# Z columns of a two-layer hybrid decoder: half of the contraction by a seven-product scheme

## The chip, the cores and the metric

The kernel runs on one core of one Trainium2 chip. The metric is the time of one execution in device microseconds. A core has a matrix engine (TensorE, PE; its weight loads are shown apart as PEld), a vector engine (VectorE, DVE), an activation engine (ScalarE, ACT), a general engine (GpSimd, POOL) and a synchronisation engine (SyncE, SP). Transfers are issued from the queues of SP, ACT or POOL and are carried out by 16 DMA engines that all queues share. SBUF holds tiles in 128 partitions; PSUM holds the results of matmuls, in eight banks of 128x512 f32.

## The reference, cut to what matters

256 tokens of width 2048 go through two layers. The second layer is an mLSTM; its input projection has columns for q and k, v, og (an output gate), z (a second gate) and two small gates. What the change touches is z and what is done with it:

```
hn  = rmsnorm(h, o_norm)
u   = hn @ o_w_in                       # [256, 2048] x [2048, 8208]
z   = u[..., 6144:8192]                 # 2048 columns
yc  = head_rmsnorm(mlstm(q, k, v, li, lf), c_norm) * sigmoid(og) * silu(z)
h   = h + yc @ o_w_out
pl  = rmsnorm(p[1] @ ple_w[1], ple_norm[1])
h   = h + sigmoid(h @ ple_gate_w[1]) * pl
out = rmsnorm(h, final_norm)
```

All is f32 with a tight tolerance, so the kernel makes each f32 product out of three matmuls of reduced precision.

## The kernel before, in words

**Products.** Every operand x is split into a high part (x rounded to the format of the fast matmul, made by a copy on ACT, L135 for weights) and a low part (x minus the high part, made on DVE, L136). A product is then high by high, high by low and low by high, three matmuls into the same PSUM bank (L196, L197, L198 in `quarter_tok`).

**Weights.** A weight matrix lies in HBM in blocks of 512 rows by 512 columns, 1 MB each, so that a block is one quarter `kq` of the contraction of one chunk `j` of columns. `load_weights` fetches a block in two halves of 512 KB through SP's queue into `raw` (five buffers, L132), and splits each half into `whi` and `wlo` (four buffers each, that is two blocks). The splits stand 400 places ahead in the order of their engines.

**A chunk.** `project_tok` walks over the four quarters; `quarter_tok` multiplies a block with both halves of the tokens (`hf`, 128 tokens each, stationary operand 128x128 from `act`, moving operand 128x512): 12 matmuls for each half, 24 for a block. After the first half `pump()` takes one step in every open lane of side work. The lanes are generators; what a step issues is queued behind the last matmul, cast and subtraction traced so far.

**The stage in question.** In the second layer the order is: q and k (`oqk`, 4 chunks), v (`ov`, 4), og (`oog`, 4), z (`oz`, 4), the embedding product `pw1` (L320), the output projection `oo`, the gate `g1`. The mLSTM itself runs in the lane "mix" beside `ov` and `oog`; its results `nums` wait in SBUF. For each of the four z chunks `gate_tok` evicts two PSUM banks: ACT makes tanh with the token's norm as scale (L522), DVE makes (tanh + 1) times z (L523), then two multiplications by the norm factor and `nums` (L1181). `feature_major` then turns the result from tokens to features: two transposes on DVE (L495), a store to DRAM and four reads back through POOL's queue (`across`, L482 and L485), a scaling on ACT (L513), and a split (L149 on ACT, L150 on DVE) into `y`, the operand of `oo`.

**The residual.** `hq`, four tiles of 128x1024, holds the layer's residual. It fills the four buffers of the pool `hp` (tag "h") from the end of the first layer until `out_proj` adds to it (L403). `ple_gate` writes it last; the lanes "fg0" to "fg3" turn it into `acth`, the operand of all four projections.

**Order.** A planner orders the instructions of each engine and each DMA queue by priority when the program is built; on the chip every engine and every queue works in that fixed order, and an instruction that waits holds what stands behind it on its engine. PSUM tiles: pool `pm` has three banks, `px` three, `pst` two.

Of the kernel before, what the change touches and what calls it, by code (L numbers as in the profile page):

```python
# [11 lines left out]
F32 = mybir.dt.float32  # L12
F32R = mybir.dt.float32r
# [30 lines left out]
def trunk(ctx: ExitStack, tc: tile.TileContext, a, out):  # L44
# [19 lines left out]
    def start(lane, gen):  # L64
        lanes.setdefault(lane, []).append(gen)
# [92 lines left out]
    def tokens(x, k, hf):  # L158
        return x[:, k, hf * P:(hf + 1) * P]
# [25 lines left out]
    def quarter_tok(w, j, kq, act, ps):  # L185

        parts = load_weights(w[4 * j + kq])
        for hf in range(2):
            for kk in range(4):
                k = kq * 4 + kk  # L190
                hi, lo = parts[kk // 2]
                c = (kk % 2) * 512
                ah, al, _ = act[k // 2]
                xh, xl = (tokens(x, k % 2, hf) for x in (ah, al))
                wh, wl = hi[:, c:c + 512], lo[:, c:c + 512]
                te.matmul(ps[hf], xh, wh, start=(k == 0), stop=False)  # L196
                te.matmul(ps[hf], xh, wl, start=False, stop=False)  # L197
                last["pe"] = te.matmul(ps[hf], xl, wh, start=False, stop=(k == KT - 1)).ins  # L198
            if hf == 0:
                pump()  # L200

    def newton(y, t, r, yh):
        v.tensor_scalar(t.bitcast(I32), y.bitcast(I32), 1, None, op0=ALU.logical_shift_right)
# [766 lines left out]
    with tc.tile_pool(name="m1", bufs=2) as m1:  # L970
# [188 lines left out]
                start("mix", mix_norm())  # L1159
        y = {}  # L1160
        held = []
        for j in range(4):
            ps = project_tok(a["oog"], j, acth)
            th = m1.tile([P, 2, 512], F32, name="tho", tag="vt", bufs=6)
            for hf in range(2):
                s.activation(th[:, hf], ps[hf], AF.Tanh, scale=norm["rth"][:, hf:hf + 1])
            held.append((j, th))
            if j == 3:
                drain("mix")
            for jj, th in [x for x in held if x[0] in nums]:  # L1170
                v.scalar_tensor_tensor(nums[jj], th, 1.0, nums[jj], op0=ALU.add, op1=ALU.mult)
            held = [x for x in held if x[0] not in nums]
        pact = load_p()
        for j in range(4):
            u = m1.tile([P, 2, 512], F32, name="u", tag="vt", bufs=6)
            gate_tok(a["oz"], j, acth, u)
            for hf in range(2):
                for i in range(2):
                    c = hf * 8 + 2 * j + i
                    e = slice(i * 256, (i + 1) * 256)  # L1180
                    v.scalar_tensor_tensor(u[:, hf, e], u[:, hf, e], fac[:, c:c + 1], nums[j][:, hf, e],  # L1181
                                           op0=ALU.mult, op1=ALU.mult)
            start(f"fm{j}", feature_major(u, "cn", 4 * j, y, 5))


        pairs = []
# [249 lines left out]
```

## Time and profile before

| What | Value |
|---|---|
| Median of 3 runs | 1035.66 us (1035.63 to 1035.77) |
| Span of the profiled execution | 1033.5 us, first to last instruction |
| Median less span | 2.2 us |
| TensorE busy | 1024.3 us, 99% of the span |
| VectorE busy | 739.6 us, 72% |
| ScalarE busy | 600.1 us, 58% |
| GpSimd busy | 90.3 us, 9% |
| Share of PE in the chain that ended last | 98% |
| z chunks, first matmul to the embedding's first matmul | 752.5 to 839.6 us |

The page gives no time of its own for the profiled execution beside its span. A busy engine is one with an instruction in work; matmuls overlap, so their durations add up to more than the time they take, and the distance between starts is what one costs. The chain that ended last is followed back from the last instruction, at each step to what released it.

### The profile page before, as it was taken

The numbers are of one execution on the slowest core, as the hardware profiler recorded it, in microseconds if no ns is written. First come the engines' busy times: TensorE is split into PE (matmuls) and PEld (weight loads), VectorE is DVE, ScalarE is ACT, GpSimd is POOL, SyncE is SP. The second block draws the span as 40 slices with busy tenths as digits, with TensorE's granted clock in tenths as the row PEclk, the third lists the DMA queues.
The fourth block names the chain that finished last, engine by engine and source line by source line (L and its number), as shares of the span: only waits on it lengthen the run. The fifth ranks groups of instructions, "written<-read, shape, count | busy, mean of one in ns | idle before, by whom it ended". The sixth has DMA issues, their size and how long they took to land.

```text
span 1033.5 us, 14411 instructions
## 1 busy us (share of the span) xinstructions
PE 1024.3 (99%) x5230; PEld 851.2 (82%) x5230; DVE 739.6 (72%) x1130; ACT 600.1 (58%) x863; POOL 90.3 (9%) x170
## 2 busy tenths in 40 slices
PE   9999999999999999999999999999999999999996
PEld 8888888888888888888888888888888888888886
DVE  7858968969685776767569986755557776766684
ACT  7675555586964444565557875654445557344562
POOL 0111101011111111111021000000001111111000
PEclk9999999999999999999999999999999999999999
DMA  9987756567688897697597655456567777788652
GB/s 364 327 238 238 224 165 204 185 195 240 227 258 296 274 282 235 213 276 230 191 268 244 221 184 173 155 180 194 187 201 228 250 252 247 221 286 269 202 184 82
DMA packets 67656, 234.79 MB, mean 227 GB/s; under 512 B 8801, under 2 KB 10209, under 8 KB 67585
## 3 DMA queue, kind: packets, MB, share of 16 engines
q1 hardware_dynamic: 55584, 196.51, 58.3%
q0 software_dynamic: 11568, 36.84, 12.5%
q8 instruction: 41, 0.67, 0.3%
q10 hardware_dynamic: 432, 0.52, 0.1%
q14 instruction: 31, 0.25, 0.1%
HBM read 216.02 MB, written 17.83 MB: 226 GB/s over the span
## 4 chain that ended last, share of the span: by engine, by line
PE 98%; ACT 1%; DMA 1%; DVE 0%; issue 0%; ACTq 0%
PE mm L196 27%; PE mm L197 27%; PE mm L198 27%; PE mx L198 4%; PE mx L197 4%; PE mx L196 4%; PE mm L320 1%; PE nu L1118 1%; DMA raw<-in_pw_dram 1%; PE mm L1262 1%; PE mm L1261 1%; PE mm L1260 1%; PE mx L632 0%; PE mx L756 0%; PE mx L1098 0%; ACT whi L135 0%
## 5 line engine op out<-in xcount | busy, mean ns | idle before, releaser
L136 DVE TENSOR_TENSOR wlo<-raw,whi 128x1024 fp32r<-128x1024 f32 (+1 forms) x357 | 431.3, 1215 | 222.0 <-ACT whi L135 209.5
L135 ACT CAST whi<-raw 128x1024 fp32r<-128x1024 f32 (+1 forms) x357 | 373.5, 1049 | 323.8 <-PE mm L198 265.7
L196 PE MATMUL mm<-whi,ahl 128*128 128x512 f32 x1216 | 474.8, 391 | 0.0
L197 PE MATMUL mm<-wlo,ahl 128*128 128x512 f32 x1216 | 473.6, 389 | 0.1
L198 PE MATMUL mm<-whi,ahl 128*128 128x512 f32 x1216 | 473.2, 389 | 0.0
L196 PEld LDWEIGHTS mm<-whi,ahl 128*128 128x128 f32 x1216 | 228.3, 188 | 48.0 <-issue 0.8
L197 PEld LDWEIGHTS mm<-wlo,ahl 128*128 128x128 f32 x1216 | 228.3, 188 | 47.5 <-DVE wlo L136 0.9
L198 PEld LDWEIGHTS mm<-whi,ahl 128*128 128x128 f32 x1216 | 228.3, 188 | 47.4
L196 PE MATMUL mx<-whi,ahl 128*128 128x512 f32 x160 | 62.2, 389 | 0.0
L197 PE MATMUL mx<-wlo,ahl 128*128 128x512 f32 x160 | 62.2, 389 | 0.0
L198 PE MATMUL mx<-whi,ahl 128*128 128x512 f32 x160 | 62.2, 389 | 0.0
L197 PEld LDWEIGHTS mx<-wlo,ahl 128*128 128x128 f32 x160 | 30.0, 188 | 6.3
L196 PEld LDWEIGHTS mx<-whi,ahl 128*128 128x128 f32 x160 | 30.0, 188 | 6.3
L198 PEld LDWEIGHTS mx<-whi,ahl 128*128 128x128 f32 x160 | 30.0, 188 | 6.1
L482 POOL DMA_DIRECT2D ducn<-w x4 | 2.2, 560 | 214.7 <-DVE w L495 214.7
L995 DVE SCALAR_TENSOR_TENSOR qk<-xr,prm,qk 128x255 f32<-128x255 f32 (+2 forms) x48 | 20.4, 471 | 0.1
L150 DVE TENSOR_TENSOR ahl<-xr,ahl 128x512 fp32r<-128x512 f32 x24 | 16.3, 685 | 4.5 <-ACT ahl L149 4.4
L149 ACT CAST ahl<-xr 128x512 fp32r<-128x512 f32 x24 | 14.7, 612 | 4.2 <-DVE xr L844 4.0
L366 DVE STREAM_TRANSPOSE w<-hq 128x512 f32<-128x512 f32 x24 | 16.7, 702 | 0.2
L384 DVE TENSOR_TENSOR ahl<-r,ahl 128x128 fp32r<-128x128 f32 x64 | 13.9, 279 | 2.9 <-ACT ahl L382 2.9
L320 PE MATMUL mm<-whi,ahl 128*128 128x512 f32 x48 | 14.9, 389 | 0.0
L382 ACT CAST ahl<-r 128x256 fp32r<-128x256 f32 x32 | 10.6, 402 | 7.5 <-DMA r<-dfo 4.7
(332 smaller groups left out, 827.5 us busy)
## 6 DMA issues: line engine op xcount, KB each, us to landing
raw<-in_ew_dram SPq DMA_DIRECT2D x64, 512.0 KB, 5.5
raw<-in_g_dram SPq DMA_DIRECT2D x64, 512.0 KB, 4.7
raw<-in_eo_dram SPq DMA_DIRECT2D x32, 512.0 KB, 5.5
raw<-in_oqk_dram SPq DMA_DIRECT2D x32, 512.0 KB, 4.7
raw<-in_ov_dram SPq DMA_DIRECT2D x32, 512.0 KB, 4.2
raw<-in_oog_dram SPq DMA_DIRECT2D x32, 512.0 KB, 4.0
raw<-in_oz_dram SPq DMA_DIRECT2D x32, 512.0 KB, 4.4
raw<-in_oo_dram SPq DMA_DIRECT2D x32, 512.0 KB, 4.8
```

The costliest lines, as they stand in the source:

```text
L135: last["act"] = s.copy(h, r).ins
L136: last["dve"] = v.tensor_tensor(out=l, in0=r, in1=h.bitcast(F32), op=ALU.subtract).ins
L149: (v.tensor_copy if name == "p0" else s.copy)(hi, src)
L150: v.tensor_tensor(out=lo, in0=src, in1=hi.bitcast(F32), op=ALU.subtract)
L196: te.matmul(ps[hf], xh, wh, start=(k == 0), stop=False)
L197: te.matmul(ps[hf], xh, wl, start=False, stop=False)
L198: last["pe"] = te.matmul(ps[hf], xl, wh, start=False, stop=(k == KT - 1)).ins
L320: last["pe"] = te.matmul(ps[hf][:, o:o + w_], tokens(pact[x], k, hf), (hi, lo)[y][:, k * 512 + o:k * 512 + o + w_], start=(n == mine[0]), ...
L366: v.transpose(w5[:, hf], h[:, hf].rearrange("p (c j q) -> p c j q", c=4, j=4))
L382: s.copy(hk, src)
L384: v.tensor_tensor(out=lk[:, hf], in0=src[:, hf], in1=hk[:, hf].bitcast(F32), op=ALU.subtract)
L995: v.scalar_tensor_tensor(dst[:, sh:T], pi[:, 0:T - sh], pc("ccw", k * 16 + n), dst[:, sh:T], op0=ALU.mult, op1=ALU.add)
```

## The change

The four z chunks are worked in two pairs (chunks 0 and 1, then 2 and 3). Quarters 2 and 3 of the contraction go on as before (`plain`, 24 matmuls a block). Quarters 0 and 1 of both chunks of a pair form a product of 2x2 blocks: two halves of tokens by two quarters, times two quarters by two chunks. These eight block products become seven (`seven`), by sums of blocks on both sides.

On the weights' side the sums are made in SBUF: the chain tile X is loaded with block (chunk 0, quarter 0), and then (1, 0), (1, 1) and (0, 1) are added to it by transfers from POOL's queue that accumulate into their destination; Y is loaded with (1, 1), and (1, 0) is added. Between two additions the present value is split into high and low parts. On the activations' side `combos` makes four combinations once, from `acth`, in a lane beside `oog`, and keeps them split in four tiles `q4`, which take the four buffers of `hp`. So `hq` is stored to DRAM after `ple_gate` and read back after the z chunks. The results are put together by partial sums in four tiles `pr` (one ACT copy and six DVE operations a pair), and the gate's operations read three of four results from SBUF instead of PSUM.

```
+    def product(o, stat, parts, first=False, end=False):
+        for k in range(4):
+            xh, xl = (x[:, k] for x in stat)
+            wh, wl = (x[:, (k % 2) * 512:(k % 2 + 1) * 512] for x in parts[k // 2])
+            for n, (x, y) in enumerate(((xh, wh), (xh, wl), (xl, wh))):
+                last["pe"] = te.matmul(o, x, y, ...).ins
+    def combos(act, qs):
+        def whole(i, j):
+            x = tp.tile([P, 512], F32, name="xr", tag="hn", bufs=3)
+            for b in range(2):
+                h, l = act[2 * j + b][0:2]
+                o = x[:, b * T:(b + 1) * T].rearrange("p (k t) -> p k t", k=2)
+                v.tensor_tensor(out=o, in0=tokens_of(h, i), in1=tokens_of(l, i), op=ALU.add)
+            return x
+        def keep(n, x):
+            q = hp.tile([P, 1024], F32R, name="q4", tag="h")
+            s.copy(q[:, 0:512], x)
+            v.tensor_tensor(out=q[:, 512:1024], in0=x, in1=q[:, 0:512].bitcast(F32), op=ALU.subtract)
...
+    def seven(w, j, act, qs, room, rest):
...
+        def add(chain, b, kq):
+            for hf in range(2):
+                gp.dma_start(out=chain[hf], in_=src(b, kq, hf), accum_op=ALU.add)
...
+        X = begin(0, 0, room)
+        parts = split(X)
+        add(X, 1, 0)
+        product(A, quadrant(act, 0, 0), parts, True)
+        p1 = part()
+        urgent(s.copy, p1, A)
+        Y = begin(1, 1, room)
+        parts = split(Y)
+        add(Y, 1, 0)
+        product(E, qs[4], parts, True)
+        plain(w, j, 2, act, (A, F), first=(False, True))
+        parts = split(X)
+        add(X, 1, 1)
+        product(B, qs[1], parts, True)
+        p15 = part()
+        urgent(v.tensor_tensor, out=p15, in0=B, in1=p1, op=ALU.add)
+        plain(w, j, 3, act, (A, F))
+        parts = split(X)
+        add(X, 0, 1)
+        product(B, qs[2], parts)
+        g = part()
+        urgent(v.tensor_tensor, out=g, in0=B, in1=p1, op=ALU.subtract)
+        parts = load_weights(w[4 * j + 1])
+        product(A, quadrant(act, 1, 0), parts, end=True)
+        yield 0, 0, A
+        pump()
+        parts = split(Y)
+        product(B, qs[3], parts)
+        urgent(v.tensor_tensor, out=p15, in0=B, in1=p15, op=ALU.subtract)
+        parts = split(X)
+        product(F, quadrant(act, 1, 1), parts, end=True)
+        urgent(v.tensor_tensor, out=p15, in0=F, in1=p15, op=ALU.subtract)
+        yield 0, 1, p15
+        pump()
+        plain(w, j + 1, 2, act, (E, B))
+        plain(w, j + 1, 3, act, (E, B), end=True)
+        urgent(v.tensor_tensor, out=g, in0=E, in1=g, op=ALU.add)
+        yield 1, 0, g
+        urgent(v.tensor_tensor, out=p1, in0=B, in1=p1, op=ALU.subtract)
+        yield 1, 1, p1
...
     acth = ple_gate(hq, a["g0"], act, pls, rp0, hss0, "on", "fg", ready(act, "fe"), gate_sums)
+    away = []
+    for c in range(4):
+        d = dr.tile([P, 2, 512], F32, name=f"dh{c}")
+        gp.dma_start(out=d, in_=hq[c])
+        away.append(d)
...
+        qs = {}
+        start("combos", combos(acth, qs))
         for j in range(4):
             ps = project_tok(a["oog"], j, acth)
...
+        drain("combos")
         pact = load_p()
-        for j in range(4):
-            u = m1.tile([P, 2, 512], F32, name="u", tag="vt", bufs=6)
-            gate_tok(a["oz"], j, acth, u)
-            for hf in range(2):
+        for jj in (0, 2):
+            us = [m1.tile([P, 2, 512], F32, name="u", tag="vt", bufs=6) for _ in range(2)]
+            for b, hf, src in seven(a["oz"], jj, acth, qs, chain_room, part_room):
+                j, u = jj + b, us[b]
+                with tc.high_priority(offset=100):
+                    s.activation(u[:, hf], src, AF.Tanh, scale=norm["rth"][:, hf:hf + 1])
+                    v.scalar_tensor_tensor(u[:, hf], u[:, hf], 1.0, src, op0=ALU.add, op1=ALU.mult)
...
+                if hf:
+                    start(f"fm{j}", feature_major(u, "cn", 4 * j, y, 5))
+        hq = []
+        for c in range(4):
+            t = hp.tile([P, 2, 512], F32, name="hq", tag="h")
+            gp.dma_start(out=t, in_=away[c])
+            hq.append(t)
```

X and Y lie in the four buffers of the tag "qk" (`chain_room`); the products of a pair run in the order P1 (X with one block), Y1, quarter 2 of chunk j, X2, quarter 3 of chunk j, X3, quarter 1 of chunk j, Y2, X4, and quarters 2 and 3 of chunk j + 1.

More of the change, by code (lines that the diff above doesn't have):

```diff
@@ L200, in quarter_tok, with split_weights @@
                 pump()
+    def split_weights(r):
+        hi, lo = (wp.tile([P, 1024], F32R, name=n, tag=n) for n in ("whi", "wlo"))
+        with tc.high_priority(offset=400):
+            last["act"] = s.copy(hi, r).ins
+            last["dve"] = v.tensor_tensor(out=lo, in0=r, in1=hi.bitcast(F32), op=ALU.subtract).ins
+        return hi, lo
+    def product(o, stat, parts, first=False, end=False):
[3 more added lines that the diff above has]
+            for n, (x, y) in enumerate(((xh, wh), (xh, wl), (xl, wh))):
+                last["pe"] = te.matmul(o, x, y, start=(first and k + n == 0), stop=(end and k == 3 and n == 2),
+                                       skip_group_check=True).ins
```

52 lines of the change are left out of this document (51 added, 1 removed).

## The prediction

> **What bounds the kernel now.** I read the busy shares on the page first, then the chain that ended last and the granted clock.
>
> ```profile
> span 1033.5 us, 14411 instructions
> PE 1024.3 (99%) x5230; PEld 851.2 (82%) x5230; DVE 739.6 (72%) x1130; ACT 600.1 (58%) x863; POOL 90.3 (9%) x170
> PE 98%; ACT 1%; DMA 1%; DVE 0%; issue 0%; ACTq 0%
> core 0: 1033.5 us, clock 0.998
> ```
>
> TensorE is busy 99% of the span at full clock and is 98% of the chain, so a matmul taken away is worth its spacing as long as nothing else makes PE wait. What one is worth, and where the z columns lie, comes from the groups by line between 752.7 and 839.6 us, two rows of the timeline of PE, and one row of the chain in order of time.
>
> ```profile
> L196 PE MATMUL mm<-whi,ahl 128*128 128x512 f32 x128 | 49.8, 389 | 0.0
> 768.01 0.39 PE L196 MATMUL mm<-whi,ahl 128*128 128x512 f32 x1
> 773.45 0.39 PE L196 MATMUL mm<-whi,ahl 128*128 128x512 f32 x1
> 839.57 10.88 PE mm L320 x48
> ```
>
> The 389 ns overlap. From 768.01 to 773.45 there are 24 starts, so a matmul costs 0.2267 us. L196, L197 and L198 have 128 each: 384 matmuls, 87.05 us, which run without a gap from 752.5 to the first L320 at 839.57. Now the other engines in that stage, in four stretches of one chunk each: PE, PEld, DVE, ACT, POOL busy us (instructions), clock, DMA share, GB/s.
>
> ```profile
> 752.70:774.50 21.80, 21.80 (x98) 18.06 (x97) 12.56 (x13) 9.75 (x11) 0.00 (x0) 1.00 0.62 194
> 774.50:796.20 21.70, 21.70 (x98) 17.96 (x97) 14.00 (x17) 9.66 (x11) 2.74 (x5) 1.00 0.78 242
> 796.20:818.00 21.80, 21.80 (x98) 18.06 (x97) 15.08 (x19) 12.39 (x17) 2.74 (x5) 1.00 0.80 241
> 818.00:839.60 21.60, 21.60 (x97) 17.90 (x96) 14.80 (x19) 12.09 (x16) 2.74 (x5) 1.00 0.77 242
> sum 86.90, PE 86.90 PEld 72.00 DVE 56.44 ACT 43.89 POOL 8.22; mean PE 21.73 PEld 18.00 DVE 14.11 ACT 10.97 POOL 2.06
> ```
>
> DVE has 30 us of room in the stage, ACT 43, and the transfers run at 0.6 to 0.8 of the engines. These three pay for the change.
>
> **PE: what goes.** Per pair of chunks, 16 products of 12 matmuls become 15; no other matmul is added. Twelve per pair, 24 in all, by 0.2267 us: 5.44 us (2.72 per pair). A product is 2.72 us, a pair 40.8 instead of 43.5, the stage 81.6. This is the whole possible gain, 0.53%.
>
> **Splits.** Per pair, 8 blocks of weights were split (two halves each); now 11, since a Strassen block serves one product instead of two. The cost of one, from the groups by line of the stage and the timeline of DVE:
>
> ```profile
> L135 ACT CAST whi<-raw 128x1024 fp32r<-128x1024 f32 x34 | 35.9, 1055 | 37.3 <-PE mm L198 37.2
> L136 DVE TENSOR_TENSOR wlo<-raw,whi 128x1024 fp32r<-128x1024 f32 x32 | 38.6, 1218 | 28.2 <-ACT whi L135 26.7
> 774.67 2.32 DVE L136 TENSOR_TENSOR wlo<-raw,whi 128x1024 fp32r<-128x1024 f32 x2
> 772.40 0.69 DVE L523 SCALAR_TENSOR_TENSOR u<-u,mm 128x512 f32<-128x512 f32 x1 [1.20 <-ACT u L522]
> 773.12 0.88 DVE L1181 SCALAR_TENSOR_TENSOR u<-u,fac,num 128x256 f32<-128x256 f32 x2
> 801.42 0.65 DVE L150 TENSOR_TENSOR ahl<-xr,ahl 128x512 fp32r<-128x512 f32 x1
> L403 DVE TENSOR_TENSOR hq<-mm,hq x12: 679/684/692, 335.6 to 938.4; 128x512 f32<-128x512 f32 x12
> ```
>
> The casts idle for PE's L198: each waits only for a slot of whi, four slots being two blocks. So a half is ready 1.06+1.22 = 2.28 us after PE lets its slot go. Six more blocks are 12 halves: ACT 12.7, DVE 14.6 us (13.9 back to back, 1.16 each). The partial sums add six DVE operations per pair between PSUM and SBUF, nearest L403: 12 by 0.684 is 8.2, and one ACT copy per pair. DVE then has 56.4+14.6+8.2 = 79 us in 81.6, ACT 58. On average DVE just fits; the narrow place is the four single products in a row (X3, kq1 of j, Y2, X4), 10.9 us. There DVE has 8 halves by 1.16 (9.3), two partial sums (1.4) and the first token half's gate (0.69+0.88): 12.2. The 1.3 over is covered by lead: a slot is free 1.5 products (4.08 us) before its half is due, which leaves 1.8. In the second pair fm0's sixth step falls on the explicit pump after kq1 and brings two of L150, 1.3, into the same place: 0.8 over. I take 0.2 for the first pair and 0.8 for the second, **1.0 us**; ends are 0 (all absorbed) and 5.2 (both pairs exceed by the whole 1.3+1.3, twice).
>
> **Activation combinations, spill, reload.** Work in the stages before and after, from the groups by form of DVE and the stretches by window:
>
> ```profile
> L384 DVE TENSOR_TENSOR ahl<-r,ahl 128x128 fp32r<-128x128 f32 x64 | 13.9, 279 | 2.9 <-ACT ahl L382 2.9
> 690.00:710.00 20.00, 20.00 (x90) 16.54 (x89) 9.31 (x8) 9.02 (x9) 0.00 (x0) 1.00 0.64 202
> 485.01 2.19 POOL L485 DMA_DIRECT2D r<-dfg  x4 [3.41 <-DMA dfg<-w]
> 518.13 0.56 POOL L482 DMA_DIRECT2D dqk<-w  x1 [30.93 <-DVE w L978]
> ```
>
> The combinations are 8 adds of 128x256 (between 0.28 and 0.68, say 0.45) and 8 operations of 128x512 (0.68): 9 us of DVE, once for both pairs, in the stage whose DVE is busy 9.3 in 20: no cost; without that cover 9 us. The spill is four stores of 512 KB on POOL's queue behind the last of fg's reads at 485; POOL's next issue is dqk at 518, after 31 idle us. The reload is asked for when the q4 tiles are free, about 13 us before the z columns end, and first read over 40 us later. On POOL it stands ahead of fm3's transfer, which is due only at the last quarter of oo's first chunk. Both cost nothing unless they slow SP's loads, which have five buffers; bounds 0 to 2 us. On SP's queue the second pair's first loads wait until X4 and Y2 are split (25 to 27 us into the first pair) and are split themselves from 34 on; behind them stand that pair's kq2 and kq3, due later still.
>
> **The accumulating transfers** are the unknown. Per pair four blocks, two 512 KB transfers each, on POOL's queue; each waits for the split that read the old value, and the next split waits for it. From the DMA issues, a stretch at the program's head and the timeline of POOL:
>
> ```profile
> raw<-in_oz_dram SPq DMA_DIRECT2D x32, 512.0 KB, 4.4
> ducn<-w POOLq DMA_DIRECT2D x4, 512.0 KB, 3.4
> row<-in_rows_dram POOLq DMA_DIRECT2D x6, 512.0 KB, 7.6
> xt<-in_x_dram SPq DMA_DIRECT2D x4, 512.0 KB, 9.4
> 8.00:16.00 8.00, 8.00 (x37) 6.54 (x35) 5.21 (x8) 7.02 (x13) 0.00 (x0) 1.00 1.02 410
> 801.79 0.56 POOL L482 DMA_DIRECT2D ducn<-w  x1 [16.07 <-DVE w L495]
> 805.80 2.18 POOL L485 DMA_DIRECT2D r<-ducn  x4 [3.45 <-PE mm L198]
> ```
>
> How long may one take? Count from the pair's first product. P1 0, Y1 2.7, kq2 5.4, X2 10.9, kq3 13.6, X3 19.0, kq1 21.8, Y2 24.5, X4 27.2, then kq2 and kq3 of j+1 to 40.8. X2's slots come free in Y1's product, so its halves are split by 6.4 and 7.7. X4's must begin to be split by 24.9 and 26.3 (2.28 before use). Between lie 18.5 us, less X3's own split 2.3: 16.2 for two adds, **8.1 us each** from issue to landing. The first add of the chain has more room (X1's split ends near -3, X2 is due at 8.6). Beyond 8.1, each us costs 2 per pair, 4 in all; the gain of 4.4 is gone at 9.2.
>
> Bounds: below by a plain SP load in this stage, 4.4 (not below: the bytes are the same); above by the slowest plain 512 KB that the run shows, xt with 9.4, plus 1.3 us for the destination (a sum has to read what it adds to: 0.52 MB at 410 GB/s): 10.7, which costs 10.4 us. I take the load 4.4 plus 1.3, plus 1.4 because the halves follow one another 1.36 us apart and share the queue: **7.1 us**, no stall. I choose the oz row as the nearest because its source, shape and stage are the same; row's 7.6 comes from pairs issued together beside small packets.
>
> DMA load: the stage moves 20.0 MB now (the four GB/s by their lengths). Six more block transfers of 1.05 MB make 26.3 in 81.6 us, 322 GB/s against 410 at the head: fits. The Trainium skill ("Collectives: The Full Stack", Stop ④) describes an add inside a transfer as read-read-write. By that eight adds read 8.4 MB more: 34.7 MB, 425 GB/s by that rule, above what the head sustained, and the sum would be that of the first rival; no row of this kernel shows an add.
>
> The sum: -5.44 + 1.0 = -4.4. The profiled execution's span is 1033.5, so 1029.1 there; the median of the runs is 1035.66, 2.2 above the span, so **1031.2**.
>
> **The rivals.**
> (1) *The adds land late; slower.* Place: X3, then X4. The point of decision is 9.2 us from issue to landing. For it: xt's 9.4 under full queues, and the destination's bytes would bring the stage to the head's rate. Against: loads here land in 4.4. At 10.7: 1031.2 + 4 x 2.6 = 1041.6; at 12, 1046.8. A POOL queue in which X3's add stands behind a transposition's reads (issue to reads 4.0, plus 2.18) adds up to 6 us in the second pair alone.
> (2) *DVE becomes the bound.* 79 us in 81.6 is 97%. If its order costs 3 to 6% the stage is 82 to 84 and the upper end of 5.2 applies: 1035.4, no change. For it: partial sums and gates need PSUM quickly and sit among the splits. Against: measured busy times overlap by 5% back to back.
> (3) *The change doesn't do what it says:* a spare matmul or a PE gap at the stage's ends takes half the gain, 1033. Against: 15 products can be counted in the code.
>
> **How the numbers follow.** 0.2% is 2.07 us, about what can be told from no change. The forecast, with (3) and small stalls (1030 to 1033.5), 0.50. Rival 2, or adds at 8.7 to 9.7 (1033.6 to 1037.7), 0.18. Rival 1, 0.32, of which 0.1 above 1045. The range 1030 to 1045 leaves out that 0.1 and a few hundredths below. The forecast's own range is 1030 to 1033.5.
>
> **What would show it.** Right: 360 matmuls of 0.2267 between the first z matmul and L320's successor, 81.6 to 83 us; chain still PE; POOL's adds landing under 8.1 us; DVE near 95% there. Wrong: weight loads of PE waiting for the split of X3 or X4, whose cast waits for the accumulating transfer (rival 1); or waiting for DVE's split while ACT's cast was long done (rival 2); a slower oqk or oo stage would contradict the spill at nothing.

## The result, and the profile after

| | Before | After |
|---|---|---|
| Median | 1035.64 us | 1048.31 us (1046.24 to 1051.18) |
| Ratio to before, 95% interval | | 1.0123 (1.0103 to 1.0143) |
| Span of the profiled execution | 1033.5 us | 1047.9 us |
| z chunks, first matmul to the embedding's first | 87.05 us | 97.18 us |
| Embedding, first matmul to the output projection's first | 10.88 us | 11.90 us |

The change made the kernel slower by 1.2%, where 0.4% faster was forecast. From the page of the changed kernel: the span, the busy engines, the issues of the accumulating transfers (count, KB, median us to landing), and the shares of the chain that ended last.

```profile
span 1047.9 us, 14475 instructions
...
PE 1025.5 (98%) x5206; PEld 848.4 (81%) x5206; DVE 764.6 (73%) x1170; ACT 613.6 (59%) x881; POOL 109.3 (10%) x194
...
PE 78%; issue 12%; DMA 6%; ACT 1%; DVE 1%; POOL 1%; ACTq 0%; POOLq 0%; SPq 0%; DVEq 0%
...
ch<-in_oz_dram POOLq DMA_DIRECT2D x16, 512.0 KB, 7.1
```

PE has its 24 matmuls less (5206 for 5230), yet its share of the chain fell from 98 to 78%. DMA has 6% of the chain now, and 12% are put down to "issue", time in which the engine waited for nothing that the profile shows. The fourth row is a trap: the median landing of the 16 accumulating transfers is 7.1 us, by chance to the digit what the prediction took for each, and the stage still lost 15.6 us against the 81.6 that 360 matmuls need.

The timeline of PE in the changed kernel shows where. Rows: start, us, instruction, and in brackets the idle time of the engine before it and what ended it.

```profile
754.91 0.39 PE L216 MATMUL mm<-whi,ahl 128*128 128x512 f32 x1
...
776.86 0.50 PE L216 MATMUL mm<-wlo,q 128*128 128x512 f32 x1 [0.76 <-DVE wlo L207]
...
817.28 0.39 PE L216 MATMUL mx<-whi,ahl 128*128 128x512 f32 x1
824.84 0.80 PE L216 MATMUL mm<-whi,q 128*128 128x512 f32 x1 [7.18 <-ACT whi L206]
826.11 0.79 PE L216 MATMUL mm<-wlo,q 128*128 128x512 f32 x1 [0.47 <-DVE wlo L207]
...
831.04 0.40 PE L216 MATMUL mm<-whi,ahl 128*128 128x512 f32 x1
...
838.58 0.50 PE L216 MATMUL mx<-wlo,ahl 128*128 128x512 f32 x1 [1.35 <-DVE wlo L207]
...
852.09 0.39 PE L457 MATMUL mm<-whi,ahl 128*128 128x512 f32 x1
```

L206 and L207 are the cast and the subtraction of the chain tiles, so these are the splits of X3 and X4. X3 of the first pair costs 1.3 us (between 775 and 777), X3 of the second pair 7.3 us (817.28 to 824.84, where 0.23 is due), X4 of the second pair 1.6. And X3's 12 matmuls then take 6.20 us (824.84 to 831.04) instead of 2.72, of which 0.47 is one more wait, for a subtraction. The cast that PE waited for, in ACT's timeline, and its cause in the chain of waits:

```profile
823.75 1.04 ACT L206 CAST whi<-ch 128x1024 fp32r<-128x1024 f32 x1 [13.14 <-DMA ch<-in_oz_dram]
```

```profile
810.63 0.56 POOL ch L284
811.19 15.37 DMA ch<-in_oz_dram
```

ACT sat idle 13.14 us until an accumulating transfer landed; the transfer of the other half was in flight for 15.37 us. Why X3's two additions were asked for only at 810.6 is seen in POOL's timeline of the second pair:

```profile
801.39 0.85 POOL L284 DMA_DIRECT2D ch<-in_oz_dram  x1 [2.63 <-DVE wlo L207]
805.49 2.26 POOL L622 DMA_DIRECT2D r<-ducn  x4 [3.25 <-DMA ducn<-w]
807.74 0.94 POOL L284 DMA_DIRECT2D ch<-in_oz_dram  x1
810.07 0.58 POOL L619 DMA_DIRECT2D ducn<-w  x1 [1.39 <-DVE w L632]
810.63 1.79 POOL L284 DMA_DIRECT2D ch<-in_oz_dram  x2
```

Y's second addition (807.74) stood behind a transposition's four reads, which waited for their store to land; X3's two stood behind the next chunk's store, which waited for its transpose. X2 had been split by 807.4, so they were 3.3 us late at the start. The landing itself, first of all 16, then by the time of issue X3 of the first pair (762 to 766) and X3 of the second (810 to 813):

```profile
DMA to landing us min/median/max: 5.6/7.1/15.4
...
DMA to landing us min/median/max: 7.7/9.4/11.0
...
DMA to landing us min/median/max: 13.0/14.2/15.4
```

Four windows of the changed kernel, two with additions in flight, one with the first pair's gap and one with the second's (last three columns: granted clock, DMA share, GB/s):

```profile
762.00:774.00 12.00, 12.00 (x55) 9.94 (x54) 5.38 (x5) 3.16 (x3) 2.55 (x3) 1.00 1.04 279
805.00:817.00 12.00, 12.00 (x54) 9.94 (x54) 7.71 (x11) 2.27 (x3) 5.55 (x8) 1.00 1.04 246
770.00:780.00 10.00, 9.12 (x40) 6.96 (x39) 6.24 (x6) 6.22 (x7) 1.70 (x2) 1.00 0.87 216
820.00:830.00 10.00, 4.69 (x9) 2.94 (x10) 3.49 (x3) 4.39 (x5) 3.92 (x7) 0.52 0.95 193
```

The DMA engines are full at 246 to 279 GB/s, where the head of the program reached 410 at nearly the same share (1.02). In the last row the granted clock is 0.52: that is most of why X3's matmuls took 6.2 us. The Trainium skill ("TensorE: Matmul & The Clock Gate", Part 1) says that an idle window of about 3.4 us puts the clock to half. This trace fits that: 0.52 comes after a gap of 7.2 us, and the first pair's gap of 1.3 us left the clock at 1.00 (third row). Two of the runs below do not: where the transposition was kept away the clock went to 0.50 (818.3 to 820 us) after a gap of 2.0, and with one pair spaced it stayed at 1.00 (840 to 850 us) through gaps of 3.4 and 2.0. So the length of a gap does not tell by itself.

Of the span's 14.4 us, 10.1 lie in the z chunks and 1.0 in the embedding. The stage also began at 754.91 instead of 752.5. That comes in the main from the head of the program, where nothing was changed: from 6 to 12 us the granted clock was 0.72 in this profile and 1.00 in that of before. In the runs below the start moves between 752.0 and 754.3, so I do not count these 2.4 us to the change. The last 0.9 lie behind.

### The profile page after: what moved, and what is told of

It is laid out like the page before. It is cut to its first block, busy times and chain, and to the rows that moved or that the text cites. A ratio compares the mean times of both kernels' runs of the same rounds, so it can differ in the third digit from the quotient of the medians.

```text
span 1047.9 us, 14475 instructions
## 1 busy us (share of the span) xinstructions
PE 1025.5 (98%) x5206; PEld 848.4 (81%) x5206; DVE 764.6 (73%) x1170; ACT 613.6 (59%) x881; POOL 109.3 (10%) x194
## 4 chain that ended last, share of the span: by engine, by line
PE 78%; issue 12%; DMA 6%; ACT 1%; DVE 1%; POOL 1%; ACTq 0%; POOLq 0%; SPq 0%; DVEq 0%
PE mm L196 20%; PE mm L197 20%; PE mm L198 20%; DMA ch<-in_oz_dram 4%; PE mx L197 3%; PE mx L196 3%; PE mx L198 3%; PE mm L216 2%; DMA hq<-dh 1%; DMA r<-ducn 1%; PE mm L1423 1%; PE mm L1422 1%; PE mm L1421 1%; PE mx L457 1%; PE mm L457 1%
## 5 line engine op out<-in xcount | busy, mean ns | idle before, releaser
L136 DVE TENSOR_TENSOR wlo<-raw,whi 128x1024 fp32r<-128x1024 f32 (+1 forms) x345 | 415.7, 1215 | 187.4 <-ACT whi L135 176.2
L135 ACT CAST whi<-raw 128x1024 fp32r<-128x1024 f32 (+1 forms) x345 | 359.7, 1047 | 284.8 <-PE mm L198 221.5
L196 PE MATMUL mm<-whi,ahl 128*128 128x512 f32 x1088 | 425.1, 391 | 0.2 <-ACT pl L469 0.2
L197 PE MATMUL mm<-wlo,ahl 128*128 128x512 f32 x1088 | 423.5, 389 | 0.0
L198 PE MATMUL mm<-whi,ahl 128*128 128x512 f32 x1088 | 423.4, 389 | 0.0
L196 PEld LDWEIGHTS mm<-whi,ahl 128*128 128x128 f32 x1088 | 204.2, 188 | 43.8 <-issue 0.8
L198 PEld LDWEIGHTS mm<-whi,ahl 128*128 128x128 f32 x1088 | 204.3, 188 | 42.6
L197 PEld LDWEIGHTS mm<-wlo,ahl 128*128 128x128 f32 x1088 | 204.3, 188 | 41.5
L207 DVE TENSOR_TENSOR wlo<-ch,whi 128x1024 fp32r<-128x1024 f32 x24 | 28.7, 1220 | 26.0 <-ACT whi L206 25.7
L206 ACT CAST whi<-ch 128x1024 fp32r<-128x1024 f32 x24 | 24.9, 1050 | 31.4 <-DMA ch<-in_oz_dram 23.6
L216 PE MATMUL mm<-whi,ahl 128*128 128x512 f32 x128 | 40.9, 389 | 0.0
L284 POOL DMA_DIRECT2D ch<-in_oz_dram x16 | 13.9, 893 | 179.7 <-DVE wlo L207 179.7
L216 PE MATMUL mm<-whi,q 128*128 128x512 f32 x64 | 23.1, 422 | 7.3 <-ACT whi L206 7.2
L216 PEld LDWEIGHTS mm<-whi,ahl 128*128 128x128 f32 x128 | 24.0, 188 | 5.0
L216 PE MATMUL mm<-wlo,ahl 128*128 128x512 f32 x64 | 25.0, 391 | 0.7 <-DVE wlo L136 0.7
```

Of the source, the lines that this page charges most:

```text
L135: last["act"] = s.copy(h, r).ins
L136: last["dve"] = v.tensor_tensor(out=l, in0=r, in1=h.bitcast(F32), op=ALU.subtract).ins
L206: last["act"] = s.copy(hi, r).ins
L207: last["dve"] = v.tensor_tensor(out=lo, in0=r, in1=hi.bitcast(F32), op=ALU.subtract).ins
L216: last["pe"] = te.matmul(o, x, y, start=(first and k + n == 0), stop=(end and k == 3 and n == 2), skip_group_check=True).ins
L284: gp.dma_start(out=chain[hf], in_=src(b, kq, hf), accum_op=ALU.add)
```

## The experiments

Theory: the landing of the additions on the chain X1 to X4 costs the time. Rivals: VectorE's load; the extra traffic of spill and reload; the total load of the DMA engines. In every table "z" runs from the first product's first matmul to the embedding's first, "gaps" adds up the places in z at which a matmul started more than 0.3 us later than the spacing of 0.2267 us gives; what z has beyond its floor and these gaps are matmuls at a lower clock and small delays. Ratios are to the kernel before, with 95% intervals. z without a gap would be 81.6 us for two pairs by seven, 84.3 for one.

| Run | Median us | Ratio | z us | Gaps in z | Embedding us |
|---|---|---|---|---|---|
| transposition kept away | 1051.49 | 1.0148 (1.0130 to 1.0167) | 90.66 | 5.7 | 13.67 |
| plain loads, same queue | 1041.46 | 1.0052 (1.0033 to 1.0071) | 91.08 | 7.0 | 11.90 |
| plain loads, SP | 1038.37 | 1.0017 (1.0004 to 1.0031) | 86.25 | 4.0 | 13.21 |
| first pair alone | 1038.79 | 1.0024 (1.0014 to 1.0033) | 89.86 | 4.9 | 10.88 |
| spill alone | 1035.94 | 1.0005 (0.9996 to 1.0015) | as before | 0 | 10.88 |
| additions on GpSimd | 1053.38 | 1.0169 (1.0150 to 1.0188) | 101.04 | 16.0 | 13.28 |
| queue written out | 1041.32 | 1.0054 (1.0035 to 1.0072) | 88.87 | 6.2 | 12.63 |
| eleven plain blocks | 1037.95 | 1.0014 (1.0005 to 1.0024) | 85.34 | 3.2 | 14.10 |
| no additions | 1032.91 | 0.9973 (0.9964 to 0.9982) | 81.60 | 0 | 13.06 |
| no additions, less DVE | 1031.58 | 0.9963 (0.9950 to 0.9976) | 81.60 | 0 | 10.88 |
| one pair, queue written out | 1037.40 | 1.0018 (1.0008 to 1.0028) | 88.52 | 3.5 | 11.88 |
| spaced, two pairs | 1051.49 | 1.0147 (1.0132 to 1.0162) | 82.06 | 0 | 19.47 |
| spaced, one pair | 1039.10 | 1.0031 (1.0020 to 1.0041) | 84.33 | 0 | 16.61 |
| **spaced, one pair, late scaling** | **1033.32** | **0.9974 (0.9965 to 0.9983)** | 84.32 | 0 | 10.88 |
| spaced, two pairs, early store | 1047.62 | 1.0110 (1.0093 to 1.0127) | 85.96 | 3.9 | 18.22 |

**Transposition kept away.** The lanes fm0 and fm1 start only after the second pair's last addition.

```
-                    start(f"fm{j}", feature_major(u, "cn", 4 * j, y, 5))
+                    late.append((j, u))
+                if jj and hf:
+                    for n, x in late:
+                        start(f"fm{n}", feature_major(x, "cn", 4 * n, y, 5))
```

> The transpositions of the first pair (fm0, fm1) start only after the second pair's last addition has been issued, so POOL's queue holds nothing but additions (and reloads of hq) while additions are pending. Theory A (POOL's queue): X3 of the second pair is late because its two additions stand behind a DRAM store, four reads and Y's addition; then its gap of 7.3 us and the slow clock behind it go, the second pair loses no more than the first (about 2.4 us), the z stage falls from 97.2 to about 86.5, the time to about 1036 to 1038. Theory B (engines): an addition occupies the DMA engines about twice as long as a load and they are full; the landing stays above 10 us, the stage above 91, the time above 1042. Theory C (DVE): no change, since DVE's work is the same.

z fell from 97.18 to 90.66: with POOL's queue free, the second pair's gaps at X3 shrink from 7.3 and 1.0 us to 2.0 and 1.0. X3's two additions there were no longer held on the queue and still landed after 10.4 and 13.0 us, as theory B has it. And oo now waits for `y` (gaps ending at ACT L149 and DVE L150 of 1.7, 1.8 and 3.0 us and smaller ones), so the total rose. The queue is one part of the cause; 5.7 us of gaps are left without it.

**Plain loads instead of additions**, on the same queue, and then on SP's. The sums are left out: X and Y are overwritten by each block.

```
-                gp.dma_start(out=chain[hf], in_=src(b, kq, hf), accum_op=ALU.add)
+                gp.dma_start(out=chain[hf], in_=src(b, kq, hf))
```
```
+                sy.dma_start(out=chain[hf], in_=src(b, kq, hf))
```

> The sixteen additions become plain loads by the same queue into the same tiles (the sums are left out, so z is another one). Theory A: POOL's order is untouched, so the second pair's X3 is still asked for 3 us late and lands behind the store; half of the loss or more stays, 1041 or above. Theory B: without the second read the engines have room, landings fall from 7.1 (median) to 5 to 6 us and from 13 to 15 to under 9 for the second pair's X3; the stage falls to 82 to 85, the time to 1032 to 1036. Theory C: still 1048.

> The sixteen additions become plain loads by SP's queue (the sums are left out). This takes away both the second read and POOL's queue. A and B: no load is late, stage near 81.6 to 83, time 1031 to 1033 if the rest of the prediction's sum holds (DVE 1.0, spill and combinations nothing). Theory C: the stage stays above 90. What is left above 1030.2 is the price of DVE, spill and combinations together; a wait on SP's in-order queue can add some.

With plain loads (median landing 4.8 us) the first pair has no gap; the second still loses 7.0 us on POOL's queue, at X3 (2.4, 1.0, ...) and X4 (1.6), and 4.0 on SP's. The second pair's X3 loads landed after 8.6 and 11.2 us on POOL's queue and after 10.0 and 11.4 on SP's, so the 1031 to 1033 us expected on SP's were missed. So two things are separate: the accumulation accounts for the first pair's gaps and part of the second's; where the transposition runs beside the chain, even plain loads are late. Part of that is POOL's order (7.0 against 4.0).

**The first pair alone** (chunks 2 and 3 by eight products).

```
-            for b, hf, src in seven(a["oz"], jj, acth, qs, chain_room, part_room):
+            for b, hf, src in (eight if jj else seven)(a["oz"], jj, acth, qs, chain_room, part_room):
```

> Only chunks 0 and 1 go by seven products; chunks 2 and 3 as before, with spill, combinations and reload kept. Gain 2.72, first pair's loss in the changed kernel's trace 1.54 + 0.84 = 2.4. A and B: 1035 to 1036.5. If spill, combinations or reload cost more than nothing the time lies above by that much; if the first pair's waits came from the second pair's loads, it lies at 1033.

Its saving is 2.7 us and its gaps 4.9: X3 costs 2.8, 0.4 and 1.0, more than in the changed kernel, and its additions landed after 11.3 and 14.0 us. The reload of `hq` moved up beside the additions here (issues at 758, 766 and 779 us); the run with one pair and the queue written out, further down, takes it away and still has 3.5 us of gaps, so the reload is at most a part of the reason. The time lies above the expected 1035 to 1036.5. No embedding loss, since chunks 2 and 3 end as before.

**Spill, combinations and reload alone**, z by eight products.

```
-            for b, hf, src in seven(a["oz"], jj, acth, qs, chain_room, part_room):
+            for b, hf, src in eight(a["oz"], jj, acth):
```

> The z columns go by eight products as before, but the four combinations are still made, hq is still stored away and read back. This prices what the prediction put at nothing. The prediction's step: 1035.7 to 1036, same. If the combinations, the spill or the reload delay loads or DVE: up to 2 us more. Nothing of the seven products is in it, so whatever it shows is common to all the other kernels.

1.0005 (0.9996 to 1.0015): they cost nothing that can be told from zero, and the embedding begins at 840.11 with no gap. This rival is out.

**Additions on GpSimd**, from blocks that SP loads; the reload deferred behind fm3.

```
-                gp.dma_start(out=chain[hf], in_=src(b, kq, hf), accum_op=ALU.add)
+                raw = wp.tile([P, 1024], F32, name="raw", tag="raw", bufs=5)
+                sy.dma_start(out=raw, in_=src(b, kq, hf))
+                gp.tensor_tensor(out=chain[hf], in0=chain[hf], in1=raw, op=ALU.add)
```

> The sums are made by GpSimd's own addition in SBUF instead of accumulating transfers; the addend is loaded by SP into a raw buffer ahead of time, so only GpSimd's addition (I estimate 2 to 3 us for 128x1024 from DVE's 1.22, as a slower engine) lies between two splits; hq is read back behind fm3's transposition. Theory B: the second read goes, loads are prefetched, the chain has 4 to 6 us where it may have 16; what is left is DVE, 1032 to 1036. Theory A: POOL's order is as in the changed kernel (stores and reads among the additions), so 4 us of the second pair stay, 1036 to 1040. If DVE's subtractions, which read two operands, are slowed by GpSimd's additions, it is above both.

The worst run. Its instructions on the chain tiles (ns min/median/max), and its groups from 745 to 860 us (busy, mean ns):

```profile
L286 POOL TENSOR_TENSOR ch<-ch,raw x16: 2388/3052/3334, 748.2 to 830.7; 128x1024 f32<-128x1024 f32 x16
```
```profile
L136 DVE TENSOR_TENSOR wlo<-raw,whi 128x1024 fp32r<-128x1024 f32 x25 | 41.4, 1686 | 3.4 <-ACT whi L135 3.3
```

DVE's subtraction takes 1686 ns in the mean, in place of 1218, in the stretch where GpSimd adds, and most gaps of PE end at DVE's L136 (4.9, 1.6, 2.0, 1.8, 1.6 us). The addition left the DMA engines and slowed the engine that had the least room.

**POOL's queue written out.** All 16 additions stand ahead of the transpositions, a store and its reads a step apart, the reload behind fm3. (Y's additions moved in the program text alone: they are split, and so added to, before X's second.)

```
-        add(Y, 1, 0)
         product(E, qs[4], parts, True)
...
         add(X, 1, 1)
+        add(Y, 1, 0)
+        gate.append(j)
...
+        if name in ("ducn0", "ducn4"):
+            while len(gate) < 2:
+                yield
```

> The additions stay as they are, but POOL's queue is put in order by hand: all sixteen additions stand ahead of every transposition, Y's behind X's second, a transposition's reads are traced one step after its store, and hq is read back behind fm3's transposition. The gate operations of the first pair are transposed in the middle of the second pair, early enough for oo. Theory A (POOL's queue and the traffic put beside the additions): the second pair loses no more than the first, 2.4 us; stage about 86.5, time 1035 to 1037. Theory B (an addition costs the DMA engines two loads, so that with the weight loads they are full and it lands in 9 to 11 us also with the queue in order): the stage stays at 88 to 90, 1038 to 1041.

z is 88.87, in theory B's range: 8.3 us of the 15.6 are gone with the order of one queue, the traffic beside the chain and the 3.5 us that X3's own matmuls had lost after the long gap. This run does not part the first two from each other. The rest stays. X3's additions, issued at once, land in 9.1 us in the first pair and 11.0 in the second (medians of the two halves):

```profile
DMA to landing us min/median/max: 7.5/9.1/10.6
...
DMA to landing us min/median/max: 9.7/11.0/12.3
```

**Eleven plain blocks.** No chain at all: each summed block is a load of its own through SP's five buffers; the sums are left out.

```
-        parts = split(X)
-        add(X, 1, 1)
+        parts = load_weights(w[4 * j + 4])
```

> The seven products without any chain: where a sum of blocks was split, a single block is loaded by SP into its own buffer ahead of time and split (the sums are left out). Eleven loads, eleven splits and all partial sums stay; no weight has to wait for another one's split. Theory C alone is left: 1031 to 1032 if DVE costs about 1 us as the prediction's sum has it; 1034 to 1036 if DVE's crowding costs 4 to 5 us. The difference to the run with plain SP loads in the chain is the price of the chain itself (load after split), to the changed kernel the price of the additions with their queue.

Still 3.2 us of gaps, in the second pair alone: 2.3 at X4 and 0.8 at the quarter behind it. Casts wait there for `raw`, up to 2.73 us: X3, kq1, Y2 and X4 use a new megabyte each 2.72 us, 385 GB/s, beside the transposition. The time is above both expected ranges.

**No additions**, X and Y are split again as loaded (the sums are left out), and the same with the 16 multiplications by the norm factor and `nums` left out too.

```
-                gp.dma_start(out=chain[hf], in_=src(b, kq, hf), accum_op=ALU.add)
+                pass
```
```
-                    v.scalar_tensor_tensor(u[:, hf, e], u[:, hf, e], fac[:, c:c + 1], nums[j][:, hf, e],
-                                           op0=ALU.mult, op1=ALU.mult)
```

> The changed kernel without its sixteen additions and with nothing in their place: X is loaded once a pair and split four times, Y twice (the sums are left out). Splits, products, partial sums, spill, reload and transpositions all stay; each pair loads seven blocks instead of the eight of before. What is left is DVE and ACT alone. If my sum's 1.0 us for DVE holds: 1031 to 1032, z stage 82 to 83. The run in which every summed block was loaded on its own took 1037.95 with casts waiting for loads in the four single products: if loads were its trouble, this one is back at 1031 to 1033; if DVE was, it stays at 1036 to 1038.

> The run without additions, and also without the multiplications by the norm factor and the mLSTM's results (16 DVE operations of 0.44 us, 7 us of DVE in the two pairs; left out). If DVE's crowding is what remains, in the second pair and in the embedding's first products behind it, this gains 2 to 4 us over the run without additions and reaches 1030 to 1031, the whole 5.44 less nothing. If it equals the run without additions, DVE was not what remained.

The window of z in the first of the two (PE, PEld, DVE, ACT, POOL busy, clock, DMA share, GB/s):

```profile
753.01:834.61 81.60, 81.60 (x361) 67.59 (x360) 72.19 (x82) 56.28 (x66) 7.73 (x14) 1.00 0.66 217
```

81.60 us without a gap: all splits, partial sums and gates are in this run, so DVE costs nothing in z as long as no weight comes late. It costs 2.2 us in the embedding (13.06 for 10.88), where the last gates stand ahead of the copies that free PSUM; with 16 DVE operations less that is gone (1031.58 us, a little above the 1030 to 1031 expected). The run without additions shows what a free addition would give: 0.9973.

**One pair, queue written out**: both edits together.

> Only chunks 0 and 1 by seven products, with POOL's queue in order: the eight additions first (Y's behind X's second), transpositions behind them, hq read back behind the third transposition and not beside the additions. Gain 2.72. In the run with both pairs and the queue in order the first pair lost 0.95 + 0.84 = 1.8, and no pair follows that the late gates could crowd. Expected 1034.9 to 1035.5, at best 0.1% faster than before. If 1037 to 1039 as in the run with one pair and the reload beside the additions, the reload was not its trouble.

1.0018 (1.0008 to 1.0028). With nothing else on POOL's queue and half the additions, X3 still has gaps of 1.3, 0.4 and 1.0 us, and its additions landed after 9.8 and 12.5. So neither the queue nor the second pair is needed for the loss, and by the sign that the expectation gave (1037 to 1039) the reload was not the main trouble of the first pair alone. How a late addition reaches PE is seen in ACT, DVE and PE at X3's first half:

```profile
771.59 1.05 ACT L206 CAST whi<-ch 128x1024 fp32r<-128x1024 f32 x1 [5.13 <-DMA ch<-in_oz_dram]
772.67 1.22 DVE L207 TENSOR_TENSOR wlo<-ch,whi 128x1024 fp32r<-128x1024 f32 x1 [4.96 <-ACT whi L206]
773.81 0.68 DVE L291 TENSOR_TENSOR pr<-mm,pr 128x512 f32<-128x512 f32 x1
774.64 0.47 PE L216 MATMUL mm<-whi,q 128*128 128x512 f32 x1 [1.12 <-DVE pr L291]
```

The cast waited for the landing and the subtraction for the cast. Behind the subtraction stood the partial sum `p15`, which reads X2's result from the PSUM bank into which X3 goes on adding, so X3's first matmul waited for that sum too, 0.7 us behind the subtraction. No run moves `p15` alone; in the run without additions it stood at the same place and cost nothing.

**The products spaced.** Either the latency of an addition on the chain or its total load on the DMA engines could be behind what is left. The next two runs keep each addition and byte of the ordered runs and change the order of the products, with one more PSUM bank, so that more work lies between two sums. Two smaller things change with it. `p15` now runs ahead of X3's split, and with two pairs the transpositions start later (first store at 841.6 us instead of 819.7; neither lies beside X3's additions).

```
-P1  Y1  kq2  X2  kq3  X3  kq1  Y2  X4  kq2'  kq3'
+P1  Y1  kq2  X2  kq2'  kq3'  X3  kq1  Y2  kq3  X4
```
```
+        F, G = (px.tile([P, 512], F32, name="mx", tag="mx") for _ in range(2))
...
+        urgent(v.tensor_tensor, out=p1, in0=B, in1=p1, op=ALU.subtract)
+        urgent(v.tensor_tensor, out=p1, in0=G, in1=p1, op=ALU.add)
```

(The primes are quarters of the other chunk of the pair, which is column j here.)

> Same additions, same bytes, ordered POOL queue as in the run with the queue written out; only the order of the products differs: P1, Y1, quarter 2 of the one chunk, X2, quarters 2 and 3 of the other, X3, quarter 1, Y2, quarter 3, X4 (one more PSUM bank, one more DVE addition a pair, the two chunks of a pair change places). Between X2 and X3 there are now 13.6 us and between X3 and X4 13.6, so an addition may take some 14.5 and 12.8 us from issue to landing instead of 8.1. Theory 1 (the landing of the additions on the chain decides, nothing else): z 81.6 to 83.5 us, no gap ahead of X3 or X4, total 1032 to 1034. Theory 2 (the additions' load on the DMA engines decides; they were busy 0.87 to 1.04 of the stage in that run): the same 88 to 90 us of z with the gaps spread over loads and additions, total 1039 to 1042.

> The same order of products, chunks 0 and 1 only; chunks 2 and 3 by eight products. Theory 1: z 84.3 to 85 us instead of 88.5 and a total of 1033 to 1035, below the kernel before by the 2.7 us of 12 matmuls less up to 2 in the embedding. Theory 2: with half of the additions the engines have room over the whole stage but not in this pair: z 86 to 88, total 1035 to 1038.

In z the first theory holds in full: no gap, 82.06 and 84.33 us. The window of z in the run with two pairs, the landing of its second X3, and its queues from 748 to 832 us (packets, MB, share of 16 engines):

```profile
752.33:834.39 82.06, 82.06 (x361) 67.42 (x360) 67.53 (x73) 51.67 (x54) 11.83 (x14) 1.00 0.94 253
...
DMA to landing us min/median/max: 11.6/12.1/12.6
...
q0 software_dynamic: 2304, 8.39, 54.0%
q1 hardware_dynamic: 3459, 12.59, 40.6%
```

These additions landed no sooner (12.1 us; 11.0 in the ordered run), the median of all 16 is 7.4, and the engines were 94% busy over the whole stage, yet PE had no gap. So latency against the distance of the sums decided, and the load alone did not. The queue rows also give the price, because q0 carried only the 16 additions here: 54.0% of 84 us by 16 engines is 726 engine-us for 8.39 MB, 87 per MB; q1's plain loads took 546 for 12.59, 43. An addition occupies the engines twice as long as a load here.

The totals missed, for a reason that neither theory had: from the embedding's first matmul to the end the two runs take 17.8 and 6.0 us longer than the kernel before. In the run with one pair, PE's rows and then ACT's:

```profile
842.15 0.50 PE L466 MATMUL mm<-whi,ahl 128*128 128x512 f32 x1 [3.24 <-DVE u L1348]
...
845.69 0.50 PE L466 MATMUL mm<-whi,ahl 128*128 128x512 f32 x1 [1.87 <-ACT pl L478]
```
```profile
840.29 0.51 ACT L666 ACTIVATE xr<-r,prm 128x256 f32<-128x256 f32 x1 [5.16 <-DMA r<-ducn]
840.71 0.67 ACT L1347 ACTIVATE u<-mm,rth 128x512 f32<-128x512 f32 x1
```

PE waits for DVE's gate of chunk 3, which waits for ACT's tanh (L1347), which stands behind chunk 2's scaling (L666), which waits for its reads. PE arrives 5 us earlier than in the run with the same queue and the old order of products, where ACT waited 1.4 us at this place and PE came later.

**The scaling behind the embedding's copies**, one pair; and for two pairs the same with chunk 0's store let in ahead of the last two additions.

```
+            if first == 8 and gain == "cn":
+                order.enter_context(tc.issue_after(last["pl"]))
```

> The spaced order for one pair, and one thing more: the scaling of chunk 2's transposed result (on ACT, before the split into y) is placed behind the embedding's copies instead of ahead of chunk 3's gate, where it waited 5.16 us for its reads and held the gate, the casts and then the embedding (gaps of 3.40 and 2.04 us in that run). Theory 1 (spacing has taken the whole price of the additions away, and what was left is this one order on ACT): z 84.3, embedding 11 to 12, total 1033 to 1034.5, below the kernel before. Rival (the DMA engines' load reaches the embedding by itself, since the engines are full at 820 to 850 too): the gaps stay at 3 to 5 us under another name and the total is 1037 to 1039.

> The spaced order for both pairs; chunk 0's transposition and store are let in ahead of the second pair's last two additions, its reads behind them, and chunk 2's scaling is placed behind the embedding's copies. In the spaced run DVE was busy 10.0 of 10 us from 820 to 850 and the gaps (3.1 <-DVE, 4.4 and 1.8 <-ACT ahl) lay in the embedding and ahead of the output projection, 12.9 us. If that was the late transposition alone: z 82, 3 to 5 us lost behind it, total 1034 to 1037. If DVE is the bound by then (80 of 82 us of work in z, and the transpositions behind it): 6 to 10 us lost behind z, total 1037 to 1042. Either way z has no gap by theory 1 unless the store costs the last two additions more than their 12.8 us.

With one pair: 1033.32 us, 0.9974 (0.9965 to 0.9983), faster than the kernel before and the changed one, with no part of the computation left out. Its page, and its window of z:

```profile
span 1031.2 us, 14451 instructions
...
PE 1021.2 (99%) x5218; PEld 848.9 (82%) x5218; DVE 756.1 (73%) x1159; ACT 609.1 (59%) x874; POOL 101.7 (10%) x186
```
```profile
752.76:837.08 84.32, 84.32 (x373) 69.82 (x372) 66.53 (x78) 50.71 (x59) 15.48 (x25) 1.00 0.89 253
```

The span is 2.3 us below before's; 12 matmuls are worth 2.7. The expectation's rival is out: from 840 to 850 us, in the embedding, the DMA engines moved 410 GB/s at a share of 1.03, and PE had no gap.

With two pairs the loss stays, and 1047.62 lies above both expected ranges: 3.9 us of gaps in z, where X4's second cast stands on ACT behind chunk 0's scaling, which waited 6.1 us for its reads, and 13.0 us more than before from the embedding to the end. In the spaced run DVE is busy 10.0, 9.9 and 10.0 of the three stretches of 10 us from 820 to 850, and gates and transpositions that it has not done in z come due in the embedding, which fits DVE as the next bound. That is argued from the busy shares; no run isolates it for two spaced pairs, and with the early store DVE was busy only 4.3 of the 10 us from 830 to 840, so it cannot be the whole reason. What costs two spaced pairs their gain stays open.

## Why the prediction was wrong

**PE, -5.44 us: right.** z without additions takes 81.60 us, exactly the forecast; with one pair spaced 84.32.

**Splits and partial sums, +1.0: too small, and the place wrong.** When no weight comes late, DVE does not make PE wait in z, in either pair; it was busy 72.2 of the 81.6 us there, where 79 were forecast. It costs 2.2 us in the embedding when z runs freely (no additions: 13.06 for 10.88), which the prediction did not look at.

**Spill, combinations, reload at nothing: right by themselves** (1.0005). The reload could still come to lie beside the additions, as in the run with the first pair alone.

**The accumulating transfers at 7.1 us, no stall: this step failed,** and in it the term for what is in flight beside an addition. Wrong was the use of one landing time for all 16. The median is 7.1, but the chain does not see the median: X3's additions, issued while Y's and the loads are in flight, took 7.7 and 11.0 us in the first pair, 13.0 and 15.4 in the second. The limit was too simple as well: 8.1 us is half of the 16.2 that X3's and X4's additions have together. X3's halves alone had 9.4 and 9.6 in the first pair (issued at 762.3 and 763.4, their casts due 2.28 us ahead of their matmuls, at 771.7 and 773.0). So the first half, at 7.7, held nothing, and the second, at 11.0, made PE wait 1.3 us. X4's additions landed in 5.6 to 5.9 us in both pairs, so "each us costs 2 per pair", which has both sums late, is not what happened either.

The first two terms, 4.4 plus 1.3, are near what an addition took with little beside it: 5.7, against those 5.6 to 5.9. Too small was the 1.4 us for sharing the queue. An addition takes the engines for twice the time of a load, so that with Y's additions and the loads in flight they were full (1.04) at 246 to 279 GB/s, and the landing became waiting time. And the clause "322 GB/s against 410: fits" was a mean of bytes over the stage. The Trainium skill ("Collectives: The Full Stack", Stop ④) calls an addition in a transfer read-read-write, and the measured 87 against 43 engine-us per MB agree with that. What the prediction hung on it, that such a load by itself brings rival 1's time, does not hold: the spaced run carried it at 94% without a gap.

**Rival 1 was what happened,** at X3, and past its 9.2 us. X4's gap in the second pair is X3's lateness handed on, since X4's own additions landed in 5.6 and 5.7 us. Its addition of "up to 6 us in the second pair alone" for POOL's queue was of the right size: on the queue itself X3's additions were 3.3 us late, and the queue written out, which moves other traffic away too, takes 8.3 us out of z. Of these 3.5 are what it did not have, the clock for the most part: after the 7.3 us gap X3's 12 matmuls took 6.2 us for 2.72. The changed kernel's 15.6 us in z are so: first pair's gaps 2.2, second pair's X3 7.3, its slow matmuls 3.5, X4 1.6, and about 1 in small pieces.

**Rival 2** (DVE) is out for z by the run without additions; for what follows two spaced pairs it stays open. **Rival 3** is out: 5206 matmuls. The limit of 8.1 itself was taken as given; it belongs to the order of products, and moving three quarters lifted it past what the additions need.

## What to carry to other kernels

Where a transfer stands in a chain of dependent steps, cost the slowest link by the traffic that is in flight beside it, not the median of its kind, and compare it with the distance that the order of work leaves; lengthening that distance was worth more here than shortening the transfer. Look at what stands ahead of a chained transfer on its queue and at what it waits for. When a stall is removed, look next at instructions that had been waiting behind it unseen: here one scaling on ACT took back the whole gain until it was moved.

## What the runs showed of the hardware that I had not expected

An accumulating transfer into SBUF costs the DMA engines 87 engine-us per MB, twice the 43 of a plain load beside it, and landed in 5.6 to 15.4 us for 512 KB in the changed kernel. With 7.2 us of idle PE the granted clock of the stretch from 820 to 830 us was 0.52; another run went to 0.50 after a gap of 2.0, and a third stayed at 1.00 through one of 3.4. A GpSimd addition of 128x1024 took 2.4 to 3.3 us and lengthened DVE's subtraction of two SBUF tiles beside it from 1.22 to 1.69 us in the mean.
